# The fourth pooling group in the front of the window attention, and the early experts' sum around the last expert

## The chip, the cores and the metric

The kernel runs on one core of one Trainium2 chip. PE is the matmul engine, DVE and ACT work on vectors, POOL and SP issue transfers. The metric is the time of one execution on the device in microseconds (us), lower is better; of several runs the median counts.

## What is computed

Two layers of a model over 256 latent tokens and 256 context tokens, 1024 wide, in float32. A layer has a mixer of four branches and a layer of 16 experts. The parts that the change touches:

```python
def pool_mix(u, pool_w, pool_scale):          # branch d: four groups of 128 columns
    ...
    for gi, w in enumerate(POOL_WINDOWS):     # windows 2, 4, 8, 16
        ...
        mean = (cs_g[:, hi] - cs_g[:, lo]) / (hi - lo)
        outs.append(mean - g[:, :, gi])
    mixed = jnp.einsum('btgc,gce->btge', pooled, pool_w)
    return mixed.reshape(b, t, POOL_W) * pool_scale

def branch_merge(h, branches, w_branch, w_gate, b_gate, w_out):
    for i, br in enumerate(branches):         # fourier, global, window, pool
        gate = jax.nn.sigmoid(h @ w_gate[i] + b_gate[i])
        merged = merged + gate * (br @ w_branch[i])
    return merged @ w_out

    for e in range(N_EXPERTS):                # moe_ffn
        hid = jax.nn.silu(tok @ w1[e]) * (tok @ w3[e])
        out = out + combine[:, e:e + 1] * (hid @ w2[e])
```

In the second layer the context tokens need no output, so its queries, pooled branch and gates cover 256 columns, against 512 in the first.

## The kernel before, in words

A float32 product is made of three float16 products (helper `mm3`, L580 to L582): high by high, low by high, high by low. A weight chunk comes from HBM into a float32 stage buffer (L219, issued by SP), ACT rounds it to `whi` (L319), DVE computes the rest `wlo` (L323). The stage buffers form a ring of four, so a chunk's transfer is issued when an earlier chunk has been split, or, for the `ada` chunks, been consumed by PE. The chunks come in the order in which the program asks for them.

Each engine executes its instructions in one fixed order. A scheduler makes that order when the program is built; the code gives it the program order, and buffers and data set the waits.

The mixer runs its attentions unit by unit: scores S on PE (L792 to L796), row maximum `mx` and its negative `nm` on DVE (L797, L806), E on ACT (L811), P on ACT and DVE (L824, L825), a transposition of P by DMA from SP's queue (L772, target `pair` in layer 0 and `pt` in layer 1), and the product with the values `po` on PE (L840). Between the steps a generator hands out other work. In the window attention it is

```python
fill = with_side(chain(spread(gated(1), pool_front(), SPREAD[l]), pool_back(), gated(3)), EV[l][1])
```

`gated(i)` computes the gates of branch i (24 products per block of 128 columns out of `h`), multiplies the branch with its weights, and adds. `spread` lets a step of `pool_front` follow every step (layer 0) or every second step (layer 1) of `gated(1)`. A pooling group (`pool_group`) takes half a weight chunk, makes 24 products, then for each sequence two copies on ACT (L941, L942), a chain of adds on DVE (L944, and L947 as often as the group's number, three times for group 3), two corrections (L951, L953), the mean (L955) and the split into `pmH` and `pmL`. `mix(g)` multiplies a group with its 128 by 128 weights on PE and writes `brH` and `brL` of branch 3 (ACT L975, DVE L976). Layer 0 has two sequences, layer 1 one. Before the change groups 0 to 2 are in `pool_front`, and group 3 runs in `pool_back`, between the mixes.

In the expert layer of layer 1 the results of the early experts go to HBM. POOL gathers them back by row (L1405) into `yg`, two buffers for each of two tiles of 128 tokens. `combine(t)` weights one on ACT (L1412), adds the other on DVE (L1413), multiplies with the layer's gate (L1415) and adds to X (L1416). The later experts' results are summed on PE in `acc` (L1339) out of `yHL`. The last expert (15) makes its two products with w1 and w3, `hidden` joins them to `sa` (DVE L1389), and the products `py` of `sa` with w2 follow in float32 (L1318). Around it stand `down(14)` and both combines.

Of the kernel before, what the change touches and what calls it, by code (L numbers as in the profile page):

```python
# [23 lines left out]
NE = 16  # L24
# [283 lines left out]
class Kernel:  # L308
# [305 lines left out]
    def mixer(self, l, nq, side):  # L614
# [3 lines left out]
        full = nq == NTOK  # L618
# [1 line left out]
        hH, hL = self.h if full else self.norm_mod(l, 1, NTOK, 0, 2)  # L620
        scope = ExitStack()
        at = Pool(scope.enter_context(tc.tile_pool(name=f"att{l}", bufs=1)),
                  {"pmH": 3, "pmL": 3, "a2": 3, "P": 3, "pt": 2 - full, "E": 3, "G": 2})

        def feat_part(ps, w, sl, n, k0, k1):
            mm3(ps[:, 0:n], lambda k: w[0][:, k, sl], lambda k: w[1][:, k, sl],
# [332 lines left out]

        def pool_front():  # L960
            pool_weights()
            for g in range(3):
                yield from pool_group(g)

        def pool_back():
            bH, bL = new_br(3)
            pwH, pwL = pooled["w"]
            psl = pooled["s"]

            def mix(g):  # L970
                pH, pL = pooled.pop(g)
                po = self.mm()
                mm3(po[:, 0:nq], lambda k: pwH[:, g, :], lambda k: pwL[:, g, :],
                    lambda k: pH[:, 0:nq], lambda k: pL[:, 0:nq], 1)
                act.activation(bH[:, g, 0:nq], po[:, 0:nq], AF.Copy, scale=psl[:, g:g + 1])  # L975
                dve.scalar_tensor_tensor(bL[:, g, 0:nq], po[:, 0:nq], psl[:, g:g + 1], bH[:, g, 0:nq],  # L976
                                         op0=ALU.mult, op1=ALU.subtract)

            mix(0)
            yield  # L980
            last = pool_group(3)
            for g in range(1, 3):
                next(last, None)
                mix(g)
                yield
            yield from last
            mix(3)
            pooled["done"] = True

        mg = self.lay.tile([128, KD, nq], F32, "merged")  # L990
# [43 lines left out]
        P = project("b", 1024)  # L1034
# [3 lines left out]
        P = project("c", 1792)  # L1038
# [41 lines left out]
    def moe(self, l, nt, side):  # L1080
# [166 lines left out]
        pe_all = ntt == 2  # L1247
# [4 lines left out]
        def experts(W, hot0, h2):  # L1252
# [197 lines left out]
            prev = more = None  # L1450
            for e in range(NE):
                pa = up(e, "w1")
                if e == NE - 1 and pe_all:
                    combine(0, True)
                if more:
                    next(more, None)
                    next(more, None)
                if prev is not None:
                    down(e - 1, prev)
                if e == NE - 1 and pe_all:  # L1460
                    combine(1, True)
                if e == NE - 1 and not pe_all:
                    fetch()
                    dw = mid["dw"] = wk.tile([128, 4, 128], F32, "dw", tag="t2")
# [11 lines left out]
                if pe_all and e > early:  # L1476
# [2 lines left out]
                            acc[t, half] = self.ps.tile([128, 512], F32, f"acc{t}{half}", tag=("mm", "pst")[half])  # L1479
                    accumulate(e - 1)  # L1480
                prev = hidden(e, pa, pb)
                if e == 1:
                    index()
                if e % EPG == 1 and e // EPG < 3:
# [101 lines left out]
```

## Time and profile before

| | us |
|---|---|
| median of 3 runs | 1464.87 (1464.43 to 1466.42) |
| profiled execution, its own time | 1468.68 |
| its span | 1466.9 |
| PE busy in it | 1352.5 (92%) |
| DVE busy | 1119.0 (76%) |
| ACT busy | 953.2 (65%) |

The span runs from the first to the last instruction of the profiled execution. A busy share is an average over stages with different limits: the 114 us in which PE is not busy lie in a small number of places. An idle time that a row shows in brackets was ended by what stands behind the arrow.

### The profile page before, as it was taken

What the parts mean: (1) busy time and instruction counts of PE and PEld (TensorE: products, weight loads), DVE (VectorE), ACT (ScalarE), POOL (GpSimd) and SP (SyncE); (2) the same over time, 40 slices, a digit from 0 to 9 for tenths busy, and PEclk for the clock granted to TensorE, in tenths of its full rate; (3) what the DMA queues carried; (4) which work ended last, traced back from release to release, by engine and by line L of the source; (5) the groups of instructions that cost most, each with busy time, mean ns of one, the idle gap of its engine ahead of it and who ended that gap; (6) DMA issues with size and microseconds to landing.
All of it is one profiled execution on the core that took longest, in us unless ns stands there. A gap on an engine that the chain in (4) does not pass through costs nothing. (4 is left out here: it accounts for less than half of the span.)

```text
span 1466.9 us, 33640 instructions
## 1 busy us (share of the span) xinstructions
PE 1352.5 (92%) x14151; PEld 927.0 (63%) x14151; DVE 1119.0 (76%) x2003; ACT 953.2 (65%) x1431; POOL 14.0 (1%) x16
## 2 busy tenths in 40 slices
PE   5999999998999998999999978899989989999984
PEld 3545454444444585777777747587768767777762
DVE  3887647877354557888988888868957888989986
ACT  3777535655233337889898655856845579899971
POOL 0000000000000000000000110000000000000010
PEclk9999999999899999999999999999999999999997
DMA  9559762797685337799999564774979779999981
GB/s 365 207 131 226 228 207 87 198 232 202 187 340 191 120 111 259 270 337 419 397 420 380 222 248 177 188 234 116 232 240 361 263 280 341 418 419 419 399 327 52
DMA packets 146416, 383.31 MB, mean 261 GB/s; under 512 B 91856, under 2 KB 93904, under 8 KB 108112
## 3 DMA queue, kind: packets, MB, share of 16 engines
q1 hardware_dynamic: 133136, 355.24, 68.8%
q10 hardware_dynamic: 11392, 19.56, 3.6%
q0 software_dynamic: 1728, 6.29, 1.2%
q8 instruction: 112, 1.84, 0.5%
q14 instruction: 48, 0.39, 0.1%
HBM read 344.88 MB, written 15.20 MB: 245 GB/s over the span
## 5 line engine op out<-in xcount | busy, mean ns | idle before, releaser
L580 PE MATMUL mm<-hH,whi 128*128 128x96 f16 (+2 forms) x1824 | 398.5, 261 | 3.3 <-ACT whi L319 2.6
L582 PE MATMUL mm<-hH,wlo 128*128 128x96 f16 (+2 forms) x1824 | 398.1, 261 | 1.0 <-DVE wlo L323 0.9
L323 DVE SCALAR_TENSOR_TENSOR wlo<-stage,whi 128x1024 f16<-128x1024 f32 (+1 forms) x212 | 318.9, 1522 | 105.0 <-ACT whi L319 104.3
L581 PE MATMUL mm<-hL,whi 128*128 128x96 f16 (+2 forms) x1824 | 398.2, 261 | 0.0
L580 PEld LDWEIGHTS <-whi 128*128 128x128 f16 x3104 | 304.9, 98 | 75.2 <-issue 4.4
L319 ACT ACTIVATE whi<-stage 128x1024 f16<-128x1024 f32 (+1 forms) x212 | 269.8, 1294 | 126.2 <-PE mm L581 87.1
L582 PEld LDWEIGHTS <-wlo 128*128 128x128 f16 x3104 | 305.0, 98 | 73.7 <-DVE wlo L323 2.7
L581 PEld LDWEIGHTS <-whi 128*128 128x128 f16 x3104 | 305.0, 98 | 72.2 <-issue 2.1
L323 DVE SCALAR_TENSOR_TENSOR wlo<-ext,whi 128x2048 f16<-128x2048 f32 x116 | 262.1, 2287 | 43.2 <-ACT whi L319 43.2
L319 ACT ACTIVATE whi<-ext 128x2048 f16<-128x2048 f32 x116 | 217.8, 1904 | 9.9 <-PE mm L582 7.4
L582 PE MATMUL mm<-xg,wlo 128*128 128x96 f16 x1024 | 132.3, 206 | 0.0
L580 PE MATMUL mm<-xg,whi 128*128 128x96 f16 x1024 | 132.3, 206 | 0.0
L581 PE MATMUL mm<-xg,whi 128*128 128x96 f16 x1024 | 132.3, 206 | 0.0
L581 PE MATMUL py<-wlo,hd 128*96 128x512 f16 x240 | 90.9, 379 | 8.9 <-DVE wlo L323 8.7
L582 PE MATMUL py<-whi,hd 128*96 128x512 f16 x240 | 90.2, 381 | 6.8 <-DVE hd L321 6.0
L580 PE MATMUL py<-whi,hd 128*96 128x512 f16 x240 | 91.0, 379 | 0.0
L580 PE MATMUL mm<-brH,whi 128*128 128x512 f16 (+1 forms) x256 | 83.5, 326 | 0.0
L582 PE MATMUL mm<-brH,wlo 128*128 128x512 f16 (+1 forms) x256 | 83.4, 326 | 0.0
L581 PE MATMUL mm<-brL,whi 128*128 128x512 f16 (+1 forms) x256 | 83.4, 326 | 0.0
L1270 PE MATMUL mm<-Dg,merged 128*128 128x384 f16 x384 | 70.3, 336 | 3.8 <-DVE Dg L1203 1.8
L500 PE MATMUL mm<-stage,cpad 128*32 128x256 f32 x768 | 58.5, 408 | 13.7 <-DMA stage<-in_w_ada_dram 13.6
L825 DVE SCALAR_TENSOR_TENSOR P<-E,rl,P 128x512 f16<-128x512 f32 (+1 forms) x96 | 59.2, 659 | 8.4 <-ACT P L824 8.2
(313 smaller groups left out, 2054.2 us busy)
## 6 DMA issues: line engine op xcount, KB each, us to landing
ext<-in_w_dram SPq DMA_DIRECT2D x118, 1024.0 KB, 9.3
stage<-in_w_dram SPq DMA_DIRECT2D x62, 1024.0 KB, 9.1
stage<-in_w_ada_dram SPq DMA_DIRECT2D x48, 1024.0 KB, 6.0
stage<-in_w_gate_dram SPq DMA_DIRECT2D x32, 1024.0 KB, 5.8
stage<-in_w_in_dram SPq DMA_DIRECT2D x16, 1024.0 KB, 6.7
stage<-in_w_branch_dram SPq DMA_DIRECT2D x32, 512.0 KB, 4.1
ydram<-ys ACTq DMA_DIRECT2D x56, 192.0 KB, 6.9
stage<-in_w_out_dram SPq DMA_DIRECT2D x8, 1024.0 KB, 6.1
```

Source lines behind the costliest of these rows:

```text
L319: a = nc.scalar.activation(hi, src, AF.Copy, scale=scale)
L323: b = nc.vector.scalar_tensor_tensor(lo, src, scale, hi, op0=ALU.mult, op1=ALU.subtract)
L500: pe.matmul(ps[32 * j:32 * j + 32, :], self.cpad[:, 2 * k:2 * k + 32], st[:, k, :], start=k < 4, stop=k >= 4, tile_position=(0, 32 * j))
L580: pe.matmul(ps, wH(k), xH(k), start=first and k == 0, stop=False)
L581: pe.matmul(ps, wH(k), xL(k), start=False, stop=False)
L582: pe.matmul(ps, wL(k), xH(k), start=False, stop=last and k == nk - 1)
L825: dve.scalar_tensor_tensor(pv[:, 1, qt, :], E[qt][:, 0:nk], r[:, qt:qt + 1], pv[:, 0, qt, :], op0=ALU.mult, op1=ALU.subtract)
L1270: pe.matmul(ps[:, 0:SLOTS], h2[n][t][:, cs(k)], Dg[:, t].rearrange("p e c -> p (e c)"), start=t == 0, stop=t == ntt - 1)
```

## The change

`pool_front` loops over all four groups, and `pmH` and `pmL` have four buffers, so that all groups can be kept until they are mixed. `pool_back` is left with the four mixes. The half chunk of weights of group 3 is asked for earlier by that. In layer 1's last expert, `combine(0)` moves from behind the w1 products to behind `down(14)`, and `combine(1)` from there to behind `hidden(15)`. No instruction is added or taken away. Behind the change the line numbers are 6 lower (L1413 is L1407, L1389 is L1383).

```diff
--- before.py
+++ after.py
@@ -620,7 +620,7 @@
         hH, hL = self.h if full else self.norm_mod(l, 1, NTOK, 0, 2)
         scope = ExitStack()
         at = Pool(scope.enter_context(tc.tile_pool(name=f"att{l}", bufs=1)),
-                  {"pmH": 3, "pmL": 3, "a2": 3, "P": 3, "pt": 2 - full, "E": 3, "G": 2})
+                  {"pmH": 4, "pmL": 4, "a2": 3, "P": 3, "pt": 2 - full, "E": 3, "G": 2})
 
         def feat_part(ps, w, sl, n, k0, k1):
             mm3(ps[:, 0:n], lambda k: w[0][:, k, sl], lambda k: w[1][:, k, sl],
@@ -959,7 +959,7 @@
 
         def pool_front():
             pool_weights()
-            for g in range(3):
+            for g in range(4):
                 yield from pool_group(g)
 
         def pool_back():
@@ -976,15 +976,9 @@
                 dve.scalar_tensor_tensor(bL[:, g, 0:nq], po[:, 0:nq], psl[:, g:g + 1], bH[:, g, 0:nq],
                                          op0=ALU.mult, op1=ALU.subtract)
 
-            mix(0)
-            yield
-            last = pool_group(3)
-            for g in range(1, 3):
-                next(last, None)
+            for g in range(4):
                 mix(g)
                 yield
-            yield from last
-            mix(3)
             pooled["done"] = True
 
         mg = self.lay.tile([128, KD, nq], F32, "merged")
@@ -1450,15 +1444,13 @@
             prev = more = None
             for e in range(NE):
                 pa = up(e, "w1")
-                if e == NE - 1 and pe_all:
-                    combine(0, True)
                 if more:
                     next(more, None)
                     next(more, None)
                 if prev is not None:
                     down(e - 1, prev)
                 if e == NE - 1 and pe_all:
-                    combine(1, True)
+                    combine(0, True)
                 if e == NE - 1 and not pe_all:
                     fetch()
                     dw = mid["dw"] = wk.tile([128, 4, 128], F32, "dw", tag="t2")
@@ -1479,6 +1471,8 @@
                             acc[t, half] = self.ps.tile([128, 512], F32, f"acc{t}{half}", tag=("mm", "pst")[half])
                     accumulate(e - 1)
                 prev = hidden(e, pa, pb)
+                if e == NE - 1 and pe_all:
+                    combine(1, True)
                 if e == 1:
                     index()
                 if e % EPG == 1 and e // EPG < 3:
```

On ACT in layer 0, at the end of the window attention, the order before was this (`stage_4380` is a gate chunk of branch 3, `E_4338` the next unit's, `poolp` are group 3's):

```order
L319 ACTIVATE adah_4308<-mm_4290 128x256
L319 ACTIVATE whi_4523<-stage_4380 128x1024
L319 ACTIVATE brH2_2938<-po_4312 128x256
L319 ACTIVATE whi_4523<-stage_4380 128x1024
L319 ACTIVATE brH2_2938<-po_4476 128x256
L319 ACTIVATE pmH_4266<-poolp_4270 128x256
L941 ACTIVATE pool0_4356<-mm_4229 128x256
L942 ACTIVATE poolp_4358<-mm_4229 128x256
L811 ACTIVATE E_4338,ls_4340<-S_4328,nm_4336 128x256
L811 ACTIVATE E_4339,ls_4340<-S_4332,nm_4336 128x256
L816 ACTIVATE es_4343<-nm_4336,sink_2757 128x2
```

Now there stands (`mm_4372` is the product of mix(3), `E_4273` the unit before `E_4354`):

```order
L319 ACTIVATE adah_4324<-mm_4304 128x256
L811 ACTIVATE E_4273,ls_4275<-S_4263,nm_4271 128x256
L811 ACTIVATE E_4274,ls_4275<-S_4267,nm_4271 128x256
L816 ACTIVATE es_4278<-nm_4271,sink_2757 128x2
L319 ACTIVATE brH2_2938<-po_4328 128x256
L975 ACTIVATE brH3_4254<-mm_4372,psl_2993 128x512
L319 ACTIVATE whi_4523<-stage_4380 128x1024
L824 ACTIVATE P_4284<-E_4273,rl_4282 128x256
L824 ACTIVATE P_4284<-E_4274,rl_4282 128x256
L811 ACTIVATE E_4354,ls_4356<-S_4344,nm_4352 128x256
L811 ACTIVATE E_4355,ls_4356<-S_4348,nm_4352 128x256
```

One unit's E, a `brH` and the fourth mix moved ahead of the split of that gate chunk, the pooling went away, and the second half of the split has moved behind the next unit's E.

On DVE in layer 1, around the last P of the window attention (`P_19014` before, `P_19063` now), the order was

```order
L998 SCALAR_TENSOR_TENSOR gate_19045<-gate_19045,mm_19096 128x256
L820 RECIPROCAL rl_19012<-ls_19005 128x2
L976 SCALAR_TENSOR_TENSOR brL3_19114<-mm_19115,psl_18401,brH3_19113 128x256
L1002 SCALAR_TENSOR_TENSOR merged_16411<-gate_19045,merged_16411 128x256
L323 SCALAR_TENSOR_TENSOR wlo_19149<-stage_18863,whi_19148 128x1024
L825 SCALAR_TENSOR_TENSOR P_19014<-E_19003,rl_19012,P_19014 128x512
L825 SCALAR_TENSOR_TENSOR P_19014<-E_19004,rl_19012,P_19014 128x512
L944 TENSOR_TENSOR pool1_19155<-pool0_19154 128x271
L976 SCALAR_TENSOR_TENSOR brL3_19114<-mm_19170,psl_18401,brH3_19113 128x256
L947 TENSOR_TENSOR pool0_19154<-pool1_19155 128x269
L976 SCALAR_TENSOR_TENSOR brL3_19114<-mm_19176,psl_18401,brH3_19113 128x256
L947 TENSOR_TENSOR pool1_19155<-pool0_19154 128x265
```

and now is

```order
L992 SCALAR_TENSOR_TENSOR gate_19096<-gate_19096,mm_19147 128x256
L820 RECIPROCAL rl_19061<-ls_19054 128x2
L976 SCALAR_TENSOR_TENSOR brL3_19163<-mm_19164,psl_18401,brH3_19162 128x256
L996 SCALAR_TENSOR_TENSOR merged_16411<-gate_19096,merged_16411 128x256
L976 SCALAR_TENSOR_TENSOR brL3_19163<-mm_19170,psl_18401,brH3_19162 128x256
L976 SCALAR_TENSOR_TENSOR brL3_19163<-mm_19176,psl_18401,brH3_19162 128x256
L825 SCALAR_TENSOR_TENSOR P_19063<-E_19052,rl_19061,P_19063 128x512
L825 SCALAR_TENSOR_TENSOR P_19063<-E_19053,rl_19061,P_19063 128x512
L323 SCALAR_TENSOR_TENSOR brL2_18274<-po_19182,brH2_18273 128x256
L976 SCALAR_TENSOR_TENSOR brL3_19163<-mm_19209,psl_18401,brH3_19162 128x256
L323 SCALAR_TENSOR_TENSOR wlo_19243<-stage_18912,whi_19242 128x1024 x2
```

The adds of group 3 (L944, L947) are gone from behind P, two L976 moved ahead of it, and the split of a chunk moved behind it. On PE there, the last 24 value products stood ahead of the last mix, 48 gate and 24 branch products in part (11 of them) and behind those in part (13); now all 24 stand behind the mixes, 48 gate and 12 branch products.

On DVE at the end, from the last splits of the weights to `sa` (L1389, now L1383), the order was

```order
L323 SCALAR_TENSOR_TENSOR wlo<-ext,whi 128x2048 x2
L1413 SCALAR_TENSOR_TENSOR yg<-yg,wr 128x1024
L323 SCALAR_TENSOR_TENSOR yHL<-py,slotw,yHL 96x512
L1415 TENSOR_TENSOR yg<-yg,merged 128x1024
L323 SCALAR_TENSOR_TENSOR wlo<-X_24636,whi 128x2048
L1416 TENSOR_TENSOR X_4729<-X_4729,yg 128x1024
L323 SCALAR_TENSOR_TENSOR yHL<-py,slotw,yHL 96x512
L1413 SCALAR_TENSOR_TENSOR yg<-yg,wr 128x1024
L1389 SCALAR_TENSOR_TENSOR sa<-mm,sa 128x384
L1415 TENSOR_TENSOR yg<-yg,merged 128x1024
```

and now is

```order
L323 SCALAR_TENSOR_TENSOR wlo<-ext,whi 128x2048 x2
L323 SCALAR_TENSOR_TENSOR yHL<-py,slotw,yHL 96x512
L323 SCALAR_TENSOR_TENSOR wlo<-X_24636,whi 128x2048
L323 SCALAR_TENSOR_TENSOR yHL<-py,slotw,yHL 96x512
L1407 SCALAR_TENSOR_TENSOR yg<-yg,wr 128x1024 x2
L1409 TENSOR_TENSOR yg<-yg,merged 128x1024
L1383 SCALAR_TENSOR_TENSOR sa<-mm,sa 128x384
L1410 TENSOR_TENSOR X_4729<-X_4729,yg 128x1024
L1409 TENSOR_TENSOR yg<-yg,merged 128x1024
```

Both halves of `yHL` and the split of the last weights (`X_24636`) moved ahead of all combining; `sa` now stands behind the additions of both tiles and one multiplication with the gate. On ACT the two weightings (L1412, now L1406) moved behind the split of `X_24636` and both `yHL`.

## Rows read from the trace of the kernel before

**Rows 1.** Waits of PE, 343 to 400: total us, times, longest.
```profile
PE S L792 <- ACT E L811: 5.1, 1, 5.1
PE mm L580 <- ACT pmH L319: 2.7, 1, 2.7
```
**Rows 2.** Timeline of PE, layer 0: start, us, engine, line, operation [idle before <- releaser].
```profile
363.50 0.37 PE L792 MATMUL S<-kH,qs 128*128 128x256 f16 x1 [5.09 <-ACT E L811]
...
369.69 0.59 PE L580 MATMUL mm<-pmH,pwH 128*128 128x512 f16 x1 [2.70 <-ACT pmH L319]
```
**Rows 3.** Timeline of ACT, layer 0, the split of the gate chunk.
```profile
359.40 1.06 ACT L319 ACTIVATE whi<-stage 128x1024 f16<-128x1024 f32 x1 [2.71 <-DMA stage<-in_w_gate_dram]
```
**Rows 4.** Timeline of SP's queue, layer 0, the issue of that chunk.
```profile
352.18 0.33 SPq L219 DMA_DIRECT2D stage<-in_w_gate_dram  x1
```
**Rows 5.** Timeline of DVE, layer 0, group 3's second sequence, first and last.
```profile
363.12 0.43 DVE L944 TENSOR_TENSOR pool<-pool 128x271 f32<-128x271 f32 x1
...
369.67 0.43 DVE L321 TENSOR_TENSOR pmL<-poolp,pmH 128x256 f16<-128x256 f32 x1
```
**Rows 6.** Windows, layer 0: length; busy us of PE, PEld, DVE, ACT, POOL; clock; DMA.
```profile
270.00:280.00 10.00, 9.32 (x61) 4.13 (x59) 9.61 (x27) 6.33 (x15) 0.00 (x0) 1.00 0.83 252
360.00:375.00 15.00, 8.21 (x30) 3.44 (x30) 11.10 (x35) 8.50 (x24) 0.00 (x0) 0.54 0.82 170
```
**Rows 7.** Timeline of PE, layer 1, end of the window attention.
```profile
1072.41 0.58 PE L840 MATMUL po<-pt,vH 128*64 128x256 f16 x3 [6.50 <-DMA pt<-P]
...
1084.76 0.28 PE L580 MATMUL mm<-hH,whi 128*128 128x256 f16 x1
```
**Rows 8.** Timeline of DVE, layer 1: a split, the last P, an L976.
```profile
1063.52 1.22 DVE L323 SCALAR_TENSOR_TENSOR wlo<-stage,whi 128x1024 f16<-128x1024 f32 x1
1064.65 1.41 DVE L825 SCALAR_TENSOR_TENSOR P<-E,rl,P 128x512 f16<-128x512 f32 x2
...
1066.33 0.48 DVE L976 SCALAR_TENSOR_TENSOR brL<-mm,psl,brH 128x256 f16<-128x256 f32 x1
```
**Rows 9.** Windows, layer 1, before and after the wait.
```profile
1030.00:1066.00 36.00, 34.99 (x333) 28.45 (x332) 36.00 (x86) 30.57 (x63) 0.00 (x0) 1.00 0.91 234
1072.00:1078.00 6.00, 5.59 (x33) 3.98 (x33) 0.71 (x2) 0.47 (x1) 0.00 (x0) 0.53 0.53 178
```
**Rows 10.** Timeline of PE, layer 1, an earlier wait.
```profile
1009.47 0.59 PE L792 MATMUL S<-kH,qs 128*128 128x512 f16 x1 [2.48 <-ACT E L811]
```
**Rows 11.** Timeline of ACT, the last expert.
```profile
1423.49 0.68 ACT L319 ACTIVATE yHL<-py,slotw 96x512 f16<-96x512 f32 x1 [0.32 <-PE py L582]
1427.83 1.15 ACT L1412 ACTIVATE yg<-yg,wr 128x1024 f32<-128x1024 f32 x1 [3.66 <-DMA yg<-ydram,late]
1428.88 1.89 ACT L319 ACTIVATE whi<-X 128x2048 f16<-128x2048 f32 x1
...
1433.69 1.15 ACT L1412 ACTIVATE yg<-yg,wr 128x1024 f32<-128x1024 f32 x1 [2.35 <-DMA yg<-ydram,late]
```
**Rows 12.** Timeline of DVE, the last expert.
```profile
1421.29 4.50 DVE L323 SCALAR_TENSOR_TENSOR wlo<-ext,whi 128x2048 f16<-128x2048 f32 x2
1432.52 1.29 DVE L1413 SCALAR_TENSOR_TENSOR yg<-yg,wr 128x1024 f32<-128x1024 f32 x1 [6.74 <-DMA yg<-ydram,late]
...
1435.51 2.28 DVE L323 SCALAR_TENSOR_TENSOR wlo<-X,whi 128x2048 f16<-128x2048 f32 x1
...
1441.75 0.56 DVE L1389 SCALAR_TENSOR_TENSOR sa<-mm,sa 128x384 f32<-128x384 f32 x1 [0.97 <-PE mm L582]
1442.23 1.22 DVE L1415 TENSOR_TENSOR yg<-yg,merged 128x1024 f32<-128x1024 f32 x1
```
**Rows 13.** Timeline of PE, the last expert's last products.
```profile
1442.41 5.60 PE L1318 MATMUL py<-stage,sa 128*96 128x512 f32 x12
```
**Rows 14.** Windows, the last expert.
```profile
1432.00:1442.00 10.00, 6.81 (x57) 4.92 (x56) 8.51 (x8) 1.51 (x2) 0.00 (x0) 0.53 0.05 20
1442.00:1444.00 2.00, 2.00 (x6) 0.73 (x5) 2.00 (x4) 0.00 (x0) 0.00 (x0) 0.77 0.00 0
```
**Rows 15.** The page's second part: busy tenths of the DMA engines in 40 slices.
```profile
DMA  9559762797685337799999564774979779999981
```

## The prediction

> **What bounds the kernel now.** I read the views in this order: the waits of PE by stretch, the timeline of PE at each long wait, then the timeline of the engine named there, and the granted clock of the stretch. PE is busy nearly everywhere else, so time can come out only where PE stands still, or where it then works at 1.2 GHz instead of 2.4.
>
> There are three such places, and the change touches each.
>
> *Layer 0, end of the window attention.* PE waits 5.1 us for one E and 2.7 us for one pmH [rows 1], at 363.50 and 369.69 [rows 2]. ACT names the cause of the first: it sat 2.71 us before the split of the gate chunk, waiting for its transfer, with E queued behind [rows 3]; that transfer had been issued at 352.18, 7.2 us earlier [rows 4]. The second wait is the fourth pooling group: its row of adds on DVE begins at 363.12 and ends at 369.67+0.43 [rows 5], and mix(3) cannot start before. Over 360 to 375 PE does 8.21 us of work at a mean clock of 0.54 [rows 6], so 8.21 x 0.46 = 3.8 us are lost besides. Together 5.1 + 2.7 + 3.8 = 11.6 us.
>
> *Layer 1, the same place.* PE waits 6.5 us for a transposed P, until 1072.41 [rows 7]; the last P ended on DVE at 1064.65 + 1.41 = 1066.06 [rows 8], 6.35 us before. DVE was busy 36.00 of 36 us before it [rows 9]: it is the late engine there. Then 5.59 us of work at 0.53 [rows 9], 2.6 us lost. Together 9.1 us.
>
> *The last expert.* ACT waits for the gathered rows with L1412, and the split of the last weights (whi<-X, 1.89 us) stands behind it [rows 11]. DVE waits 6.74 us with L1413, and the second half of the split (2.28 us) starts only at 1435.51 [rows 12]. So sa ends at 1442.31 and the last products start at 1442.41 [rows 13], after ten microseconds at a mean clock of 0.53 [rows 14].
>
> **The change, part by part.**
>
> *Group 3 into the front.* The number of instructions stays; they change place. DVE's work for the group is, per sequence and from the durations of rows 5, four adds of 0.43, two more operations of that length and a few small ones, about 3.0 us: 6.0 us in layer 0 (two sequences), 3.0 us in layer 1. Its 24 products take 24 x 0.21 = 5.0 us in layer 0 (half of that in layer 1; 34.99 us for 333 products of mostly 256 columns, 0.105 each [rows 9], twice that for 512).
>
> Layer 0: ACT now has E of the thirteenth unit, two brH and mix(3) ahead of the split of the gate chunk, as the order shows; only the next E stands behind it. The chunk is issued when the first ada chunk of this stretch is consumed. From there I replay: transfer 7.2 us as in rows 3 and 4, whi 1.06, two P 0.9, E 0.5: that E ends 9.7 us after the issue. PE has ahead of the scores that need it 23 products of 512 columns (9 of the mixes and 14 of the gate, 4.8 us) and some 3.5 us of scores, values and the ada chunk, an estimate from the same rate: 8.3 us. A wait of 1.4 us is left, against 7.8 us before; mix(3) waits for nothing, since its group is long done. The gate's products, which had stood behind the waits, are now the cover. At 1.4 us I keep the clock at full, so the 3.8 us come back too: 11.6 - 1.4 = 10.2. In exchange DVE has 6.0 us more in the front, where E is already waited for now and then; DVE has 9.61 of 10 us busy in 270 to 280 [rows 6], while the 5.0 us of products that come along cover most of it. Bounds: 0 (all covered) and 6.0 (none); I take 1.0, near the first, since PE gets almost as much work as DVE. Gain 9.2. Ends: 11.6 (no wait at all), and 11.6 - 8.9 - 6.0 = -3.3, a loss, if the old E wait (5.1 and its 3.8 of clock) stays and nothing is covered.
>
> Layer 1: the last P moves later. In front of it now stand the group's 3.0 us and two L976 more (0.96), behind it one split (1.22) [rows 8]: 1066.06 + 2.7 = 1068.8, landing 6.35 us on, 1075.1. What is next late is this same transfer, but PE now has work before it. Counting the order against the point PE had reached at 1065.9, it now does 62 products more before it asks for the transfer (48 of the gate, 12 of a branch, 3 mixes, one value fewer): 62 x 0.105 = 6.5 us, 1072.4 at the earliest. From the landing, 24 value and 12 branch products, 36 x 0.105 = 3.8 us, lead to the gate product that ran at 1084.76 [rows 7]: 1078.9, a gain of 5.9. A wait of up to 2.7 us is left, and a wait of 2.48 us in this layer was followed by matmuls of 0.59 us that last 0.38 at full clock [rows 10]; that would take back up to 2.6 us. The transfer before this one may be late as well and split the wait in two. I take 5.9, at full clock. Ends: 9.1 (all of it), and about 0 if P comes 3.0 us later still and PE then works at the low clock (5.9 - 3.0 - 2.6 = 0.3).
>
> The fourth pmH/pmL buffer keeps the group from waiting for mix(0); the space costs no time. The weight half of group 3 moves ahead of one gate or branch chunk on SP's queue in either layer. Those chunks' transfers wait for a ring slot, not for the queue, except in layer 0 as above. A late one costs what rows 3 show, 2.7 us on ACT.
>
> The Trainium skill, "DMA: Bandwidth & Descriptors", section "Anatomy of one DMA", says that DMA engines do not wait on semaphores: the wait sits on the issuing sequencer, ahead of the dispatch. Here that speaks against the change, as a weight transfer would stand behind a transposition that waits for a later P. The trace agrees in kind (the row of SP at 352.18 comes after a transposition), and the first rival below takes its price.
>
> *Combine(0) and combine(1) later.* ACT: whi<-X no longer stands behind L1412, so it can start when the yHL that began at 1423.49 ends, 1424.2, and end at 1426.1, where it ended at 1428.88 + 1.89 before [rows 11]. DVE: its half ends at about 1428.8, after the two ext splits that end at 1425.8 and one yHL. PE then has the 46 products left that took 3.9 us at low clock; at full clock 2 us: about 1431. But sa now stands behind both L1413 and one L1415 on DVE (new numbers L1407, L1409). The first waits for the gather as before, to 1432.52 + 1.29 = 1433.8; the second needs ACT's turn of 1433.69 + 1.15 = 1434.84 [rows 11, 12]; with 1.29 and 1.22 that is 1437.35, and sa ends at 1437.9 instead of 1442.31: 4.4 us sooner. The new wait, sa for the gathers, lasts 6 us, and who waits behind it is PE with the last products. The two L1416 and the other L1415, 3.65 us, now come after sa, beside 5.6 us of products; if that cover were gone, they would cost up to 3.65.
> Price: PE then starts after 5 us of standing still. The first microseconds of those products run at the low clock; before, only 2 us of them ran at 0.77 [rows 14]. If 4.5 us run at half, 2.25 are lost where 0.46 were, 1.8 more. Gain 4.4 - 1.8 = 2.6. Ends: 4.4, and -1.0 if the gathers land 3.6 us later than now.
>
> The Trainium skill, "TensorE: Matmul & The Clock Gate", section "Why this matters for your kernels", says that an idle gap between bursts of matmuls drops the clock. By it the gain here is 2.6, without it 4.4; rows 14 agree with it (0.53 after PE's waits).
>
> *Sum.* 9.2 + 5.9 + 2.6 = 17.7 us. The profiled execution took 1468.68, of which 1466.9 is the span; it gives 1451.0. The three timed runs lie 3.8 us under it (median 1464.87): 1447.2. Nothing in between should give it back, since the stretches after each place are in the same order, and their transfers are triggered by the work that comes sooner.
>
> **The rivals.**
>
> *The gate chunk is late again in layer 0.* ACT would wait for it as in rows 3, now with the fourteenth unit's E behind. For it: the transfer takes 7.2 us, only 1.4 short of PE's cover as I count it, and transpositions share the queues. Against it: it is issued after an early ada chunk, not after a split. Price: the 5.1 us and the 3.8 us of clock, 8.9 us; 1447.2 + 8.9 = 1456.1.
>
> *The expert layers are bound by their weights.* If the weight stream, not PE, sets the pace from the first expert on, what the front wins is waited for later. For it: the DMA engines are at nine tenths or more in five slices of either expert layer, the 18th to 22nd and the 34th to 38th [rows 15]. Against it: the first expert loads are issued behind the place that comes sooner, so the stream moves with it. If layer 1's 5.9 and half of layer 0's go, 1447.2 + 5.9 + 4.6 = 1457.7.
>
> *Slower: the front breaks up.* DVE is full before the last P of layer 1 [rows 9], so the group's 3.0 us delay each softmax behind it. If PE then runs out of products several times, each such wait costs what the one of 363.50 did, 5.1 us and 3.8 of clock. Two of them (17.8) eat the gain; from three on (26.7) it is slower: 1447.2 + 26.7 = 1473.9. For it: E is waited for now already, 2.48 us in one row [rows 10]. Against it: the group brings its own products.
>
> *It does not do what it says.* The scheduler could place the group as before: but the order shows group 3's work and both combines moved. What is left is that all three gains are eaten in passing: 1464.9.
>
> **How the numbers follow.** Chances: forecast 0.62 (its own range 1440 to 1453); late gate chunk 0.14; weight-bound 0.09; slower 0.07; no change 0.08. The low end is the forecast with the better ends of all three (2.4, 3.2 and 1.8), 1439.8, and a little under it: 1438. The high end takes in both middle rivals with some microseconds for their spread: 1461. That leaves about 0.15 to 0.2 out. A measurement here can tell 0.2%, 2.9 us, from no change: faster 0.86, same 0.07, slower 0.07.
>
> **What would show it.** Right: in layer 0 no wait of PE above 2 us for E or pmH, and the granted clock at full from 330 to 400; in layer 1 the wait for pt under 3 us; at the end whi<-X on ACT starts near its yHL, DVE reaches sa right after an L1409, and py starts some 4 us sooner relative to the gathers. Wrong: ACT waiting for stage<-in_w_gate ahead of an E; several new waits of S for E in the front; py not sooner; or PE waiting for ext chunks in the expert layers by what the front has won.

## The result and the profile after

| | kernel before | changed kernel |
|---|---|---|
| median, first comparison (4 runs each) | 1465.52 us | 1449.48 us (1447.53 to 1450.3) |
| ratio, 95% interval | | 0.9889 (0.9872 to 0.9906) |
| median, a later comparison (17 and 5 runs) | 1465.93 us | 1452.55 us (1450.75 to 1454.35) |
| ratio, 95% interval | | 0.9906 (0.9892 to 0.9921) |
| profiled execution, its own time / its span | 1468.68 / 1466.9 us | 1449.04 / 1447.3 us |
| PE not busy in the span | 114 us | 101 us |

By the medians the change is 16.0 us faster in the first comparison and 13.4 in the later one, by the ratios 16.3 and 13.8. The forecast was 17.7, and both medians lie in its range. The profiled spans differ by 19.6, since the profiled execution of before lay 3.2 us above the median of the first comparison and that of the changed kernel 0.4 below its own. The runs e1 to e10, which are named here already, are the experiments of the next section.

**Layer 0.** The waits of PE in the changed kernel, 343 to 400 (total us, times, longest), where before 5.1 and 2.7 stood [rows 1]:

```profile
PE S L792 <- ACT E L811: 1.2, 1, 1.2
PE mm L477 <- DVE brL L976: 0.9, 1, 0.9
```

The place on PE, on ACT and on SP's queue (start, us, engine, line, operation, idle before and what ended it), against [rows 2 to 4]:

```profile
350.30 1.07 PE L500 MATMUL mm<-stage,cpad 128*32 128x256 f32 x16
...
362.83 0.27 PE L792 MATMUL S<-kH,qs 128*128 128x256 f16 x1 [1.22 <-ACT E L811]
```
```profile
360.48 1.06 ACT L319 ACTIVATE whi<-stage 128x1024 f16<-128x1024 f32 x1 [1.06 <-DMA stage<-in_w_gate_dram]
```
```profile
349.41 5.15 SPq L772 DMA_TRANSPOSE pair<-P  x2
354.62 0.57 SPq L219 DMA_DIRECT2D stage<-in_w_gate_dram  x1
```

The wait for pmH is gone, the wait for E has shrunk from 5.09 to 1.22 us. ACT still waits for the gate chunk, 1.06 us instead of 2.71, since its transfer, issued at 354.62, lands 5.9 us later and not 7.2. The issue follows the end of two transpositions (349.41 + 5.15) by 0.06 us, and the first ada chunk, after which the prediction has it issued, had been consumed by 351.37 (350.30 + 1.07): it stood in their queue for 3.25 us. PE had products meanwhile, so at this E the price of the rival did not come.

(The Trainium skill, "DMA: Bandwidth & Descriptors", section "Anatomy of one DMA — SWDGE (gpsimd) path", says that a semaphore is waited for on the issuing sequencer, ahead of the dispatch. The rows above don't test that: what the chunk stood behind is 5.15 us of issuing, not a wait for a semaphore.) The issue at 352.18 of [rows 4], which the prediction sets beside this, shows no such queue: in the kernel before the last transposition was issued 6.3 us earlier, with two weight transfers between.

```profile
343.29 2.62 SPq L772 DMA_TRANSPOSE pair<-P  x2
```

The rival's mechanism did come, but at an earlier E, where nobody had looked for it. Another gate chunk, issued at 328.41, landed at 336.6, 8.2 us later, and ACT waited 3.61 us for it. The first row is the changed kernel's; the others are of its second profile (e5), where the chunk took 9.3 us:

```profile
336.61 2.00 ACT L319 ACTIVATE whi<-stage 128x1024 f16<-128x1024 f32 x2 [3.61 <-DMA stage<-in_w_gate_dram]
```
```profile
339.68 2.00 ACT L319 ACTIVATE whi<-stage 128x1024 f16<-128x1024 f32 x2 [5.59 <-DMA stage<-in_w_gate_dram]
```
```profile
340.77 1.23 DVE L323 SCALAR_TENSOR_TENSOR wlo<-stage,whi 128x1024 f16<-128x1024 f32 x1 [5.66 <-ACT whi L319]
341.91 0.22 DVE L806 TENSOR_SCALAR nm<-mx,nsink 128x2 f32<-128x2 f32 x1
```
```profile
342.79 0.27 PE L792 MATMUL S<-kH,qs 128*128 128x256 f16 x1 [2.21 <-ACT E L811]
```

DVE's split stands behind ACT's, nm behind DVE's split, E behind nm, and PE waits for E. In the kernel before, ACT does not wait for the chunk that is issued at about that time. In the profiles with the change in layer 0 and no added work PE's wait there is under 0.25 us where the chunk took 7.7 to 8.2 us (changed, e1, e9), 1.5 us where it took 9.1 (e6), and 2.2 where it took 9.2 or 9.3 (e4, e5). Why it takes longer in some executions no run shows.

**Windows of the changed kernel** (length; busy us of PE, PEld, DVE, ACT, POOL; clock; DMA), layer 0 and then layer 1 behind the wait, against [rows 6, 9]:

```profile
360.00:375.00 15.00, 13.79 (x89) 6.35 (x88) 9.54 (x26) 9.78 (x23) 0.00 (x0) 1.00 0.92 225
1056.00:1070.00 14.00, 13.58 (x134) 11.77 (x132) 10.47 (x16) 7.45 (x12) 0.00 (x0) 1.00 1.03 279
```

The granted clock is full in both places, where it was 0.54 and 0.53. Over 330 to 400 it is full in the changed kernel, and in e5 too, behind the wait of 2.21 us:

```profile
330.00:400.00 70.00, 67.44 (x488) 32.51 (x487) 41.95 (x112) 33.87 (x78) 0.00 (x0) 1.00 0.80 237
```
```profile
330.00:400.00 70.00, 65.33 (x478) 31.55 (x477) 41.49 (x113) 33.50 (x80) 0.00 (x0) 1.00 0.78 230
```

**Layer 1.** The last P on DVE, its transposition on SP, and the values on PE, against [rows 7, 8]:

```profile
1056.64 1.41 DVE L825 SCALAR_TENSOR_TENSOR P<-E,rl,P 128x512 f16<-128x512 f32 x2 [0.18 <-ACT P L824]
```
```profile
1058.08 3.04 SPq L772 DMA_TRANSPOSE pt<-P  x1
```
```profile
1063.13 0.38 PE L840 MATMUL po<-pt,vH 128*64 128x256 f16 x3 [0.42 <-DMA pt<-P]
...
1065.85 0.27 PE L580 MATMUL mm<-hH,whi 128*128 128x256 f16 x1
```

The wait for pt is 0.42 us instead of 6.50. The issue of the transposition took 3.04 us on SP; in the kernel before it took 4.20:

```profile
1066.09 4.20 SPq L772 DMA_TRANSPOSE pt<-P  x1
```

**The end.** ACT, DVE and PE around the last expert's sa, against [rows 11 to 13]:

```profile
1406.16 1.90 ACT L319 ACTIVATE whi<-X 128x2048 f16<-128x2048 f32 x1
...
1415.43 1.15 ACT L1406 ACTIVATE yg<-yg,wr 128x1024 f32<-128x1024 f32 x1 [4.45 <-DMA yg<-ydram,late]
```
```profile
1414.24 1.28 DVE L1407 SCALAR_TENSOR_TENSOR yg<-yg,wr 128x1024 f32<-128x1024 f32 x1 [2.86 <-DMA yg<-ydram,late]
1417.37 1.28 DVE L1407 SCALAR_TENSOR_TENSOR yg<-yg,wr 128x1024 f32<-128x1024 f32 x1 [1.84 <-DMA yg<-ydram,late]
1418.57 1.22 DVE L1409 TENSOR_TENSOR yg<-yg,merged 128x1024 f32<-128x1024 f32 x1
1419.70 0.55 DVE L1383 SCALAR_TENSOR_TENSOR sa<-mm,sa 128x384 f32<-128x384 f32 x1
...
1427.60 0.75 DVE L323 SCALAR_TENSOR_TENSOR yHL<-py,slotw,yHL 96x512 f16<-96x512 f32 x1 [3.75 <-ACT yHL L319]
```
```profile
1420.31 8.25 PE L1312 MATMUL py<-stage,sa 128*96 128x512 f32 x12 [6.04 <-DVE sa L1383]
```

DVE waits twice for gathered rows before it reaches sa, PE stands still for 6.04 us behind it, and then the twelve products take 8.25 us, where they took 5.60. The windows show the clock:

```profile
1414.00:1420.00 6.00, 0.27 (x5) 0.12 (x3) 3.92 (x4) 1.40 (x2) 0.00 (x0) 0.94 0.28 103
1420.00:1424.00 4.00, 3.69 (x5) 1.41 (x6) 3.85 (x6) 0.00 (x0) 0.00 (x0) 0.50 0.00 0
```

PE does 0.27 us of work in the six, and then works at 0.50 of the clock, the lower level.

**Place by place.** For each run the same ACT and DVE instructions as in the kernel before were paired in order; the median of their time differences says how far a run leads, and what the lead grows by across a place is that place's gain. "Without" are runs in which that place was left as before: they show the scatter of one profile.

| place | forecast | with the change there, us | without, us |
|---|---|---|---|
| layer 0 | 9.2 | 9.1 (changed), 9.8 (e1), 7.2 (e4), 7.0 (e5), 7.6 (e6), 9.5 (e9) | -0.4 (e2), 2.0 (e3) |
| layer 1 | 5.9 | 7.6 (changed), 7.6 (e2), 7.6 (e4), 7.4 (e5), 7.3 (e6), 7.3 (e9) | -0.6 (e1), 0.0 (e3), 1.7 (e8) |
| the end | 2.6 | 1.8 (changed), 2.2 (e3), 2.0 (e5), 2.0 (e7), 2.3 (e10) | 1.5 (e1), -1.3 (e2), 1.1 (e8) |

The means with the change are 8.4, 7.5 and 2.1; those without, with the zero of the kernel before itself, are 0.5, 0.3 and 0.3. The differences, 7.8 + 7.2 + 1.7, come to 16.7. The spread in layer 0 goes with the late gate chunk: 9.1 to 9.8 where PE did not wait behind it, 7.0 to 7.6 where it did.

### The profile page after: what moved, and what is told of

The parts are those of the page before. It is cut to its first block, busy times and chain, and to the rows that moved or that the text cites. A ratio compares the mean times of both kernels' runs of the same rounds, so it can differ in the third digit from the quotient of the medians.

```text
span 1447.3 us, 33640 instructions
## 1 busy us (share of the span) xinstructions
PE 1345.9 (93%) x14151; PEld 923.4 (64%) x14151; DVE 1118.3 (77%) x2003; ACT 952.8 (66%) x1431; POOL 16.5 (1%) x16
## 5 line engine op out<-in xcount | busy, mean ns | idle before, releaser
L581 PE MATMUL mm<-hL,whi 128*128 128x96 f16 (+2 forms) x1824 | 395.3, 260 | 0.0
L581 PEld LDWEIGHTS <-whi 128*128 128x128 f16 x3104 | 303.9, 98 | 71.2 <-issue 1.2
L581 PE MATMUL mm<-xg,whi 128*128 128x96 f16 x1024 | 132.3, 206 | 0.0
L581 PE MATMUL py<-wlo,hd 128*96 128x512 f16 x240 | 90.9, 379 | 8.9 <-DVE wlo L323 8.7
L581 PE MATMUL mm<-brL,whi 128*128 128x512 f16 (+1 forms) x256 | 83.4, 326 | 0.0
```

What stands on the lines that cost most here:

```text
L581: pe.matmul(ps, wH(k), xL(k), start=False, stop=False)
```

## The experiments

**The three parts one by one.** e1, e2 and e3 make one part each. In e1 the number of groups in front depends on the layer (`full` is layer 0), and in e2 the same with `not full`:

```diff
-            for g in range(3):
+            for g in range(4 if full else 3):
```

and the other layer keeps the old `pool_back` and three buffers; e3 is the kernel before with the two `combine` calls moved. The order of ACT and DVE was, in each, that of the changed kernel in its part and that of the kernel before elsewhere.

> The kernel before with the change in layer 0 alone: four buffers and group 3 in the front there; layer 1 and the last expert stay as before. Theory (the three gains are local and independent): in layer 0 the split of the gate chunk waits for its transfer by about 1 us instead of 2.7, PE's waits of 5.1 and 2.7 us go, and the equal work behind it comes 9.1 us sooner, which stays to the end: about 1456.4 us, 9 below the kernel before. Rival (bound by the weight stream): a part of the 9 us is waited for again in the expert layer of layer 0 or in layer 1; then it is 1459 to 1462, and PE has new waits for weights. Rival (layer 0's gain is given back in layer 1's attention, which waits longer for its transposition): 1460.

> The kernel before with the change in layer 1's mixer alone. Theory: the wait of 6.5 us for pt falls to 0.4, the clock behind it stays full, 7.7 us are gained there; the stretch of the router and dispatch, where 1.3 us were given back in the changed kernel, is in unchanged order: if the loss belongs to the earlier arrival, it is here too (gain 6.4, 1459.1 us); if it was a matter of that one profiled execution, 7.7 remain (1457.8 us). Rival (part of layer 1's gain comes from layer 0's, through transfers that are under way earlier): a wait for pt of 2 to 3 us is left here and the gain is 5 or less, 1460.5 us or more.

> The kernel before with the two combines moved in the last expert alone; both mixers as before. Theory: whi of the last weights starts at its yHL, sa waits about 6 us for the gathers, the last products run at half clock: gain 1.9 us, 1463.6 us. Rival (the change at the end does nothing, the 1.9 us of the profile are scatter): within 0.7 us of the kernel before. Rival (slower): the idle 6 us and the low clock cost more than what is gained: 1466 or more.

Measured against 1466.34 us, by the ratios: e1 1460.89, ratio 0.9968 (0.9955 to 0.998), 4.7 us less; e2 1458.39, 0.9945 (0.9931 to 0.9959), 8.1 less; e3 1464.9, 0.9995 (0.9985 to 1.0005), 0.7 less and no difference that can be told. Together 13.5 us (14.8 by the medians), against 13.8 and 16.3 of the whole change: the parts add up.

e2 came as its theory said (its profiled execution, 1464.09, is the slowest of its six), and its wait for pt is 0.4 us without any help from layer 0, so that rival falls.

e1 missed its 1456.4 by 4.5 us, and its time is about what both of its rivals forecast (1459 to 1462, and 1460). Its profile speaks against them: PE's waits for the split expert weights (py for wlo, L581) are 8.7 us in it as in the kernel before, the lead does not change through layer 0's experts (9.6 from 600 to 850), and the place in layer 1 takes 0.6 of it. But 1.4 us went again in the router's stretch of layer 0, whose order is unchanged. And the profiled execution of e1 (1458.17) is the fastest of its six, 2.7 us under their median, while that of the kernel before lies 2.3 over the median here. So by the time of all executions layer 0's part is 4.7 us (2.9 to 6.6), less than the 9.8 of its profile and the 7.8 of the table. Where the others lose it stays open. They may have had the late chunk's wait, which this profile has not; no trace shows it.

e3's time tells its theory apart neither from "does nothing" nor, by the interval, from "slower". Its place gain of 2.2 us is above what unchanged ends scatter to (-1.3 to 1.5), but by little.

**The end: sa first.** e4 is the changed kernel with both combines queued behind `sa` on DVE and behind the last split on ACT:

```diff
-                if e == NE - 1 and pe_all:
-                    combine(0, True)
...
                 if e == NE - 1 and pe_all:
-                    combine(1, True)
+                    with tc.issue_after(self.last_split.ins), tc.issue_after(mid["join"].ins):
+                        combine(0, True)
+                        combine(1, True)
```

> The changed kernel with both combines queued behind sa on DVE and behind the split of the last weights on ACT. Theory (sa waited for the gathers only because it was queued behind them, 6.0 us, and py ran at half clock because of that wait): sa follows the last w3 products at once, py starts with no wait and its 12 products take about 3 us instead of about 8; the combines (7.5 us of DVE from the first gather on) then end before or about when py's second half is there, and DVE's yHL comes about 3.5 us sooner than in the changed kernel: 1446 us. Rival (the end is bound by the gathers and DVE, not by sa): the combines take as long behind sa as they took ahead of it, yHL on DVE waits for them and comes as late as now: 1449 to 1450, no gain.

1449.87 us, ratio 0.9886 (0.9868 to 0.9903): no more than the changed kernel by the time, as the rival had it and not the theory, though its end gained 6.7 us (against 1.8) in the profile; ahead of the end, where the order is the same, the lead of this profile over the kernel before was 11.6 us, 6.0 less than that of the changed kernel's. On DVE, ACT and PE of e4:

```profile
1419.01 0.56 DVE L1385 SCALAR_TENSOR_TENSOR sa<-mm,sa 128x384 f32<-128x384 f32 x1 [1.63 <-PE mm L584]
1420.11 1.28 DVE L1409 SCALAR_TENSOR_TENSOR yg<-yg,wr 128x1024 f32<-128x1024 f32 x1 [0.54 <-DMA yg<-ydram,late]
1423.24 1.28 DVE L1409 SCALAR_TENSOR_TENSOR yg<-yg,wr 128x1024 f32<-128x1024 f32 x1 [1.85 <-DMA yg<-ydram,late]
1424.44 2.35 DVE L1411 TENSOR_TENSOR yg<-yg,merged 128x1024 f32<-128x1024 f32 x2
1426.71 2.35 DVE L1412 TENSOR_TENSOR X<-X,yg 128x1024 f32<-128x1024 f32 x2
```
```profile
1429.42 1.26 ACT L319 ACTIVATE yHL<-py,slotw 96x512 f16<-96x512 f32 x2 [6.35 <-DVE slotw L1293]
```
```profile
1420.09 7.06 PE L1314 MATMUL py<-stage,sa 128*96 128x512 f32 x16
```

sa now waits for PE and not for the gathers: it had only been queued behind them. PE goes on without a wait, and its products take 0.44 us each (7.06 for 16), so twelve take 5.3 us and not the 3 that was expected. But a small operation for slotw had gone behind the combines, and ACT waited 6.35 us for it. e6 mends this: slotw is made ahead of the combines, and combine(0) is finished before combine(1).

> As the run with sa first, and besides the last expert's slot weights (slotw) are made ahead of both combines, and combine(0) is done as a whole before combine(1). In the run with sa first, ACT waited 6.35 us for slotw, which stood behind both combines on DVE, and DVE idled 1.85 us for the second gather. Theory (the end is DVE's work from the first gather on, once nothing is queued wrongly): yHL no longer waits for slotw, the multiplication and addition of combine(0), 2.4 us, fill the wait for the second gather; from the first gather's landing to the end about 2.4 us less than with sa first and 7 less than in the changed kernel, about 1443 to 1445 us if the changed kernel takes 1450 here. Rival (the gain at the end is lost to the clock, as the times of the run with sa first suggest, 1449.9): 1449 to 1450, no gain.

1446.29 us, ratio 0.986 (0.9843 to 0.9876), in one comparison with e5, the changed kernel, at 0.9906 (0.9892 to 0.9921): 6.3 us less by the medians, and the intervals do not meet. The theory holds; the end gained 8.2 us in the profile, against 6.7 in e4. How much of the step is slotw's and how much is the order of the two combines was not separated. PE runs straight into its last products:

```profile
1417.73 0.29 PE L1296 MATMUL hotT<-id,Dg 128*96 128x128 f16 x2
1417.86 5.34 PE L1314 MATMUL py<-stage,sa 128*96 128x512 f32 x12
```

This version is faster than both kernels in that comparison.

**The price of the low clock.** e9 is the changed kernel with 34 products that nobody reads, queued on PE where it waits for sa:

```diff
+                    if e == NE - 1 and pe_all and half == 0:
+                        with tc.issue_after(mid["tp"].ins):
+                            for _ in range(34):
+                                pe.matmul(py[:, 0:EPG * CAP].rearrange("p (e c) -> p e c", c=CAP), self.id16[:, 0:CAP],
+                                          hot[e // EPG][:, 0], start=True, stop=True)
```

> The changed kernel with 34 products of 384 columns ahead of the last expert's first py, which nobody reads (their place in py is written anew by the real products): PE works during most of its 6.0 us of wait for sa. Every other order is that of the changed kernel. Theory (the term that was mis-sized at the end is the clock: py's twelve products took 8.25 us at half clock in the changed kernel and 5.60 in the one before): the twelve products take 5.4 to 5.6 us, and the end comes 2.6 us sooner: 1447 to 1449 us where the changed kernel takes 1449.5 to 1452.5. Rival (the products' length has nothing to do with the engine's standing still): they take 8 us again, no gain. Rival (the yHL and additions behind py wait for DVE's combines anyway): py is shorter, the end comes no sooner.

```profile
1416.14 5.69 PE L1313 MATMUL py<-Dg,id 128*96 128x384 f16 x34
1422.17 5.39 PE L1317 MATMUL py<-stage,sa 128*96 128x512 f32 x12 [0.35 <-DVE sa L1388]
```

The same twelve products, which start behind sa as before, take 5.39 us instead of 8.25, and the end gains 4.9 us in this profile instead of 1.8 to 2.3. The window over them has the granted clock at full, against 0.50 in the changed kernel:

```profile
1422.00:1426.00 4.00, 3.83 (x9) 1.55 (x10) 3.71 (x6) 0.12 (x1) 0.00 (x0) 1.00 0.02 4
```

Work in place of the wait kept the clock up behind it: here 2.9 us. By the time, 1448.32 us and 0.9886 (0.9866 to 0.9906), the gain lies within what two comparisons of the changed kernel differ by.

**The changed kernel again.**

> The changed kernel once more, beside the other three of this call. Its time against the kernel before should be 0.989 again (16 us less). What it tells apart: in the router's stretch of layer 1, whose order is unchanged, the three profiles with the change in layer 1 lost 1.3 to 3.2 us against the kernel before, the three without it 0 to 0.2. If the loss is scatter of the granted clock behind the two idle stretches there, this profile may lose 0; if it follows from the change, it loses 1.3 or more again, with the clock at 0.8 and 0.6 behind the two stretches.

The time is 0.9906 of the kernel before's and not 0.989 again. The router's stretch of layer 1 cost it 0.7 us more than the kernel before. Over all profiles it cost 0.2 to 3.2 where layer 1 is changed (mean 1.1 of eight) and 0 to 1.4 where it is not (mean 0.4 of four, the kernel before with its zero among them; the 1.4 is e8). So the loss comes without the change too, and stays away with it; whether the means differ can't be told from so few. The clock behind the two stretches in which PE has little to do falls to different depths in equal order. The same ten microseconds of the router, in the profiles of before and of the changed kernel, with the clock (third number from the end) at 0.83 and 0.66:

```profile
1180.00:1190.00 10.00, 6.41 (x35) 3.50 (x35) 9.63 (x59) 5.44 (x12) 0.00 (x0) 0.83 0.98 360
```
```profile
1161.00:1171.00 10.00, 6.21 (x31) 3.27 (x31) 9.02 (x61) 5.09 (x11) 0.00 (x0) 0.66 0.98 352
```

**How much cover the fronts have.** e7 and e10 add 7 and 21 adds on DVE to group 3 for each sequence:

```diff
+                for extra in range(EXTRA if g == 3 else 0):
+                    dve.tensor_tensor(buf[1][:, 1:T + 16], buf[0][:, 0:T + 15], buf[0][:, 1:T + 16], op=ALU.add)
```

> The changed kernel with seven more adds of 0.43 us in group 3 for each sequence (they write again what the first add wrote): 3.0 us of DVE more per sequence, 6.0 in layer 0 and 3.0 in layer 1, with no product beside them. Theory (the front of layer 0 covers DVE's work in part, the front of layer 1 hardly, since only 0.4 us of wait for pt are left and P moves 3.0 us later): layer 0 loses 1 to 3 us, layer 1 3 us and up to 2.6 for the clock: 1454 to 1459 us against 1450. Rival (the fronts have slack for a whole group more): within 1 us of the changed kernel. Rival (the front breaks up, each late E costs its wait and the clock): more than the 9 us of added work, 1460 or more.

> As the run with seven more adds, with 21: 9.0 us of DVE more per sequence, 18 in layer 0 and 9 in layer 1, with no product beside them. With seven, the places lost 0.9 us of 6.0 in layer 0 and 2.1 of 3.0 in layer 1. Theory (the front of layer 0 covers DVE's work as long as DVE has idle time around the group: 8 us of the 40 from 295 to 335 in the changed kernel; in layer 1 DVE is busy throughout): layer 0 loses about 18 - 8 = 10 us or somewhat less, layer 1 9 us and up to 2.6 for the clock: 1465 to 1472, the gain of the change is gone. Rival (the price stays what it was with seven, 1.4 us for 9): 1454 to 1456. Rival (the front breaks up, each late E costs its wait and the clock): above 1475, more than the work that was added.

e7: 1453.97 us, 0.9918 (0.9902 to 0.9934), 1.4 us over e5 by the medians and just under what I expected. e10: 1460.91 us, 0.9968 (0.9956 to 0.9979), also under the expectation. In layer 0 the place still gained 6.9 and 8.9 us, as much as without the adds (7.0 to 9.8): 18 us more of DVE cost nothing that shows. I had reckoned with the idle time of 295 to 335, but the 42 adds spread from 302.5 to 342.5 us, and what is late behind them is caught up later. The hundred microseconds around, in the changed kernel and in e10, show DVE (third busy time) 12 us fuller and PE (first) as busy as before:

```profile
275.00:375.00 100.00, 97.05 (x666) 47.16 (x664) 75.46 (x215) 58.98 (x143) 0.00 (x0) 1.00 0.77 220
```
```profile
275.00:375.00 100.00, 96.62 (x665) 46.88 (x663) 87.57 (x256) 59.04 (x143) 0.00 (x0) 1.00 0.80 215
```

In layer 1 the place gained 5.4 with 3 us more, and lost 3.1 with 9 us more: 2.1 and 10.6 from 7.5. There the expectation held (9 and up to 2.6). PE's waits of e10 in layer 1, and the window at the first:

```profile
PE mm L581 <- DVE gate L995: 7.2, 2, 5.1
```
```profile
1056.00:1068.00 12.00, 4.42 (x43) 2.97 (x42) 11.70 (x32) 7.74 (x16) 0.00 (x0) 0.79 0.58 175
```

DVE is busy 11.70 of 12 us there, and PE 4.42.

**Is the place in the front needed?** e8 is the kernel before with group 3 of layer 0 run as a whole ahead of mixes 1 to 3, behind mix(0):

```diff
+            if full:
+                yield from pool_group(3)
+                for g in range(1, 4):
+                    mix(g)
+                    yield
+            else:
...
```

Behind `else:` stand the old lines, for layer 1.

> The kernel before with one edit in layer 0: group 3 stays behind the front, after mix(0), but all of it runs ahead of the mixes 1 to 3 instead of between them; three buffers as before. Theory (two separate causes: pmH is late because the group is the last thing before mix(3), E is late because a gate chunk's split, which waits for its transfer, is queued ahead of it): the wait for pmH shrinks or goes, since the mixes 1 and 2 now stand behind the group as well, a wait of that kind moves to mix(1); E's wait of about 5 us stays somewhere: gain 0 to 3 us, 1463 to 1466. Rival (the group's place between the mixes is the one cause, moving it by a few steps is enough): both waits go, the gain in the profile is 9 us as with the change in layer 0 alone.

1463.36 us, 0.9982 (0.9972 to 0.9993), 2.6 us less; 2.6 in the place as well. The size was as expected, the way to it was not: the scheduler put E ahead of the gate chunk's split, and it was the wait for E that went. On PE:

```profile
360.01 0.27 PE L792 MATMUL S<-kH,qs 128*128 128x256 f16 x1 [1.14 <-ACT E L811]
361.56 0.30 PE L840 MATMUL po<-pair,vH 128*64 128x256 f16 x1 [1.09 <-DMA pair<-P]
367.56 0.58 PE L580 MATMUL mm<-pmH,pwH 128*128 128x512 f16 x1 [3.60 <-ACT pmH L319]
```
```profile
355.00:370.00 15.00, 9.05 (x70) 4.58 (x65) 14.01 (x50) 10.18 (x28) 0.00 (x0) 0.73 1.01 275
```

With E ahead of the split its wait is 1.14 us, as in the changed kernel, so the 5.1 us of before came from that queue. But DVE's group, 14.01 of 15 us busy, still stands where PE has no products left, and pmH is waited for longer than before. So E ahead of the split, without the group's move, brings 2.6 of the 7.8 us. The other half alone, the group in the front with that split still ahead of E, was not run.

## Why the prediction was right

*Layer 0, forecast 9.2, measured 7.8 over the scatter in the profiles, and 4.7 (2.9 to 6.6) by the time of e1.* The two old waits went as worked out, and the clock stayed full. The sum left a wait of 1.4 us for E; it was 1.1 to 1.4 us in seven profiles and 0.4 in e10. That this came so near is in part luck: counted from the ada chunk's end at 351.37, that E freed PE after 11.5 us and not 9.7, since the issue stood 3.25 us in the queue and the transfer was 1.3 us shorter than assumed, and PE arrived after 10.2 us and not 8.3. The two errors cancel. What the sum did not have is the earlier gate chunk, whose late landing cost PE up to 2.2 us and makes two profiles (e4, e5) break the prediction's own sign of being right, no wait above 2 us. For DVE's 6.0 us in the front I took 1.0 between 0 and 6.0; e10 shows no price even for 18 us more, so the cover is far larger than I knew, and the waits of 1.5 to 2.2 us for an E at 341 to 343 (e4, e5, e6) belong to the chunk and not to DVE's work.

*Layer 1, forecast 5.9, measured 7.2: the mis-sized term.* On the clock of the kernel before (the lead ahead of the place is 11.3 us), P ended at 1069.4 instead of 1068.8, its landing came at 1074.5 instead of 1075.1, 5.1 us on and not the 6.35 of [rows 7, 8] (the issue on SP was 1.2 us shorter); PE arrived at 1074.1 instead of 1072.4, so that 0.4 us of wait were left. From there to the gate product of 1084.76 it took 2.7 us and not 3.8, since the value products from the landing on, 23 of the 24, took 1.4 us (1063.13 to 1064.53), 0.06 each, and not the 0.105 that I took from a mean over mostly larger products. The landing's 0.6 and the products' 1.1 make the 1.7 us between the forecast and this profile's 7.6.

*The end, forecast 2.6, measured 1.7.* On the same clock (lead 17.6 us) sa was forecast to end at 1437.9 and ended at 1437.9 (1420.25 + 17.6), though DVE's second addition waited for its own gather and not, as in the sum, for ACT's turn; the new wait was forecast at 6 us and took 6.04; the additions behind sa were covered (DVE then idles 3.75 us). What was off is the clock's price: I put 1.8 us, and the products took 8.25 - 5.60 = 2.65 longer. e9 shows this term alone.

*The rivals.* The late gate chunk: at the E that the prediction named, ACT waited 0.4 to 1.2 us for it, and PE was covered in the main; at an earlier E it came true, but at 0 to 2.2 us, with the clock full, and not at the 8.9 of the rival. The bound by the weights: from 1200 to 1380 the lead of the changed kernel stays at 17.6 us to a tenth, through the whole expert layer; nothing was waited for again. The front that breaks up: not even with 18 us of DVE more in layer 0. No change: both comparisons lie outside 0.2% by their whole intervals.

*The rest.* The places come to 16.7 against the forecast 17.7; the time shows 16.3 and 13.8 by the ratios. A sum from one execution cannot see what stretches that nobody changed do in others: against the profile of the kernel before, the other profiles lose 0 to 3.2 us in the router of layer 1, up to 2.2 (e10) in that of layer 0, and up to 3.1 (e9) between 860 and 960. In the router of layer 1 the granted clock goes with it (0.83 and 0.66 above). That these stretches make up the difference is not shown, since only one execution of each run was profiled.

## What to carry to other kernels

Look for the last stretch in which a vector engine still has a block of work and the matmul engine has none left: move the block to where matmuls stand beside it, and make sure that nothing waiting for a transfer is queued ahead of what the matmuls need. When work is pushed behind a critical instruction, see to it that all that is critical goes ahead of it, the small operations too; moving the combines behind the last weights was worth 0.7 us as the change had it (e3, within the noise), and 6.3 more once sa and slotw stood ahead of them and one combine was finished before the other (e6). A wait of the matmul engine can cost twice: the one of 6.04 us made the products behind it 2.65 us longer, and work put into it took that back (e9).

## What was not expected of the hardware

The same transfer of a weight chunk, in the same order of instructions, took 8.2 us from issue to landing in one profile of the changed kernel and 9.3 in the other (issued at 328.41 and 330.35), and with it a wait of 2.2 us came and went. The clock is not the same in each execution either: the router of layer 1 cost up to 3.2 us more than in the kernel before's profile, with granted clocks of 0.83 and 0.66 in the two profiles shown. And products whose results nobody reads, put into a wait of 6 us, gave the following twelve 2.9 us back, 5.39 instead of 8.25 us.
